# Identity transposes ahead of the first real ones, and one coefficient load on another queue

## The chip, the cores and the metric

The kernel runs on one core of a Trainium2 chip. The metric is device time in microseconds (us) of one execution. Before the change the median of three runs is 1470.12 us.

## What is computed

One layer of an encoder for two sequences of 512 tokens with 1024 features: a norm of the rows, a wide projection, a windowed attention branch, a state-space branch, a gated merge, and an MLP. Everything is in fp32. What the change touches is the beginning:

```python
def rms_norm(x, g):
    xf = x.astype(jnp.float32)
    y = xf * lax.rsqrt(jnp.mean(xf * xf, axis=-1, keepdims=True) + EPS)
    return (y * g.astype(jnp.float32)).astype(x.dtype)
...
    h = rms_norm(x, ln1)
    proj = h @ w_in
    q, k, v, u, g_att, g_ssm = jnp.split(proj, IN_SPLITS, axis=-1)
...
    a_re, a_im, bb_re, bb_im = s5_discretize(lam_re, lam_im, log_dt, b_re, b_im)
```

The state-space branch has 64 groups of 16 channels with 64 states in two directions. `s5_discretize` turns the decay rates `lam` and `log_dt` into powers and scale factors, which are then multiplied with the coefficients `b` and `c` of each group.

## The kernel before

The 1024 rows of x (both sequences) are eight tiles `xs[0]` to `xs[7]` of 128 rows by 1024 features, 512 KB each. SyncE (SP) issues their loads (L285), four of them, then the first two halves of a weight column (`fetch`, L165), then the other four.

**The front.** `square_rows(t)` squares a tile on ScalarE with a row sum (L290), and GpSimd turns the sum into the scale of each row (L292, L293). `scale_rows(t)` multiplies the rows on VectorE (L296). `turn_rows(s, k)` transposes the k-th 128 features of the four tiles of sequence s on TensorE into one PSUM tile (L301; tiles named `sps` and `tps` in turn), so that the features lie on the partitions. From that PSUM tile ScalarE writes a rounded copy `hT[s][0]` (L303), and VectorE writes what rounding left out, `hT[s][1]` (L304). Each product of the projection is then three matmuls per k (L185): rounded by rounded, rounded by rest, rest by rounded. `split` does the same rounding for a weight half, with a cast on ScalarE (L175, tile `c_hi`) and a subtraction on VectorE (L176, tile `c_lo`), and after the second half issues the next `fetch`.

**The order.** From L270 to L436 the instructions of all five engines keep the order in which the program writes them (`manual_schedule`). After L436 this holds for TensorE and GpSimd alone (L437), and the planner orders the others; it may also put their later instructions between earlier ones of the written order. Matmuls of the projection are handed out in small portions by `pull(units)`, two units each: three matmuls after each `turn_rows(0, k)` from k = 2 on, and larger portions later.

For the first sequence the loop over k reads:

```python
        for k in range(KT):
            turn_rows(0, k)
            if k % 2 == 0:
                square_rows(4 + k // 2)
            elif k > 1:
                scale_rows(3 + k // 2)
            if k in (4, 5):
                split(k - 4)
            if k > 1:
                pull(6)
```

So ScalarE and VectorE work on the transposed tiles of the first sequence and, in between, on the rows of the second one.

**The coefficients.** `coefficients()` is a long chain of small VectorE operations (L327 to L384), handed out by `some(n)` among the rest. Its results are copied into tables (L429 to L438). Then `tables(c)` runs for eight blocks c of eight groups. It loads the block's coefficients into `bcx` (L469, 256 KB, two buffers), multiplies them with the factors (L475 to L481), forms `bpre` (L504 to L507) and `ctab` (L528 to L532), lets TensorE transpose `bpre` (L517), and stores `ctab` through GpSimd's queue (L533). `h`, which holds the states, is a tile of the pool opened after the front's pools are closed; GpSimd clears its first step (L444) ahead of the first `tables`. GpSimd's written order around there is: the row scales (L292, L293), small operations on constants (L415 to L419), the store of a line of attention biases (L423), the clearing of `h` (L444), and the stores of `ctab` (L533).

**PSUM.** `acc()` gives one of three accumulator tiles in turn, `sps()` one of two, `tps()` one of two. `ident` is the 128 by 128 identity, made by GpSimd at the start.

Of the kernel before, what the change touches and what calls it, by code (L numbers as in the profile page):

```python
# [19 lines left out]
P = 128  # L20
# [43 lines left out]
def hybrid_layer(ctx, tc, x, rel, onehot, w_qkv, w_ug, vectors, lam, coefs, w_glu, w_out, ln2,  # L64
                 w_up, w_down, out):
    nc = tc.nc
    V, S, PE, GP, SP = nc.vector, nc.scalar, nc.tensor, nc.gpsimd, nc.sync
# [12 lines left out]
    def acc():  # L80
        return ps_acc.tile([P, 512], F32, tag="acc", name="acc")

    def tps():
        return ps_t.tile([P, 512], F32, tag="tps", name="tps")

    def sps():
        return ps_s.tile([P, 512], F32, tag="sps", name="sps")
# [16 lines left out]
    ident = const.tile([P, P], F32, name="ident")  # L104
# [166 lines left out]
    with tc.tile_pool(name="xin", bufs=1, reuse_waits="tile") as xin, tc.tile_pool(name="ssmc", bufs=1) as sc:  # L271
# [23 lines left out]
        def scale_rows(t):  # L295
            V.tensor_scalar_mul(xs[t], xs[t], scales[t])  # L296

        def turn_rows(s, k):
            ps = tps() if k % 2 else sps()
            for i in range(4):  # L300
                PE.transpose(ps[:, i * P:(i + 1) * P], xs[s * 4 + i][:, k * P:(k + 1) * P], ident)  # L301
            h = hT[s][0][:, k, :]
            S.activation(h, ps, AF.Copy, scale=gain_1[:, k:k + 1])  # L303
            V.scalar_tensor_tensor(hT[s][1][:, k, :], ps, gain_1[:, k:k + 1], h.bitcast(F32),  # L304
                                   op0=ALU.mult, op1=ALU.subtract)
# [93 lines left out]
# [10 lines that stand above are left out]
        scale_rows(7)  # L409
        pull(12)  # L410
        for k in range(KT):
            turn_rows(1, k)
            pull(6)
            some(4)
# [27 lines left out]
    with tc.tile_pool(name="hst", bufs=1) as hp:  # L442
# [11 lines left out]
        with tc.tile_pool(name="ssmt", bufs=2) as sp:  # L454
# [9 lines left out]
            def tables(c):  # L464


                gs = slice(c * SB, (c + 1) * SB)
                bcx = sp.tile([P, SB, 4, CH], F32, tag="bcx", name="bcx")
                SP.dma_start(bcx, coefs[:, gs])  # L469
                bcv = bcx.rearrange("p g i c -> p i g c")  # L470
                bx, cx = bcv[:, 0:2], bcv[:, 2:4]
                bb = sp.tile([P, 4, SB, CH], F32, tag="bb", name="bb", bufs=1)
# [105 lines left out]
            for c in range(KT):  # L578
                tables(c)
                if c == 1:  # L580
                    step_factors()
# [610 lines left out]
    with tc.tile_pool(name="glu", bufs=1, reuse_waits="tile") as gpool, \  # L1192
# [10 lines left out]
        for u in range(2, 2 * KT):  # L1203
            m, s = divmod(u, 2)
# [436 lines left out]
```

## Time and profile before

| what | us |
|---|---|
| median of three runs | 1470.12 |
| the three runs | 1469.74, 1470.12, 1473.99 |
| the profiled execution's own time | 1473.9 |
| its span (first to last instruction) | 1472.1 |
| VectorE busy | 1098.8 (75%) |
| ScalarE busy | 758.3 (52%) |
| GpSimd busy | 212.2 (14%) |

A row of the timeline reads: start in us from the start of the span, duration in us, engine, line, operation, what it writes and reads, shape, how many in a row, and in brackets how long the engine had been idle before and what released it. PE is TensorE's matmul, PEld its weight load, DVE VectorE, ACT ScalarE, POOL GpSimd, and SPq, ACTq, POOLq are instructions that issue a DMA. A row of the waits reads: who waited for whom, microseconds in total, how often, the longest. A row of the windows reads: the stretch, its length, the busy time of each engine with the number of instructions, the granted TensorE clock (PEclk), the share of the DMA engines and GB/s.

### The profile page before, as it was taken

The numbers are of one execution on the slowest core, as the hardware profiler recorded it, in microseconds if no ns is written. First come the engines' busy times: TensorE is split into PE (matmuls) and PEld (weight loads), VectorE is DVE, ScalarE is ACT, GpSimd is POOL, SyncE is SP. The second block draws the span as 40 slices with busy tenths as digits, with TensorE's granted clock in tenths as the row PEclk, the third lists the DMA queues.
The fourth block names the chain that finished last, engine by engine and source line by source line (L and its number), as shares of the span: only waits on it lengthen the run. The fifth ranks groups of instructions, "written<-read, shape, count | busy, mean of one in ns | idle before, by whom it ended". The sixth has DMA issues, their size and how long they took to land.

```text
span 1472.1 us, 22149 instructions
## 1 busy us (share of the span) xinstructions
PE 1441.2 (98%) x8074; PEld 1232.5 (84%) x8074; DVE 1098.8 (75%) x1989; ACT 758.3 (52%) x1362; POOL 212.2 (14%) x372
## 2 busy tenths in 40 slices
PE   6999999999999999999999999999999999999998
PEld 4888888888999999998888878888888878888787
DVE  7989849996645899998984587777776597475553
ACT  6678852235535888786343355544554444333332
POOL 3033351002331444232100000000000000000000
PEclk9999999999999999999999999999999999999999
DMA  4455549429840445376552245444443893454441
GB/s 177 140 172 180 167 159 347 144 100 315 316 163 16 149 147 170 99 243 228 190 193 107 86 160 177 146 154 146 145 148 113 327 341 104 158 185 146 127 129 58
DMA packets 102877, 249.16 MB, mean 169 GB/s; under 512 B 12234, under 2 KB 23754, under 8 KB 102768
## 3 DMA queue, kind: packets, MB, share of 16 engines
q1 hardware_dynamic: 60240, 139.55, 29.1%
q0 software_dynamic: 16896, 53.53, 10.7%
q10 hardware_dynamic: 25632, 54.67, 10.1%
q8 instruction: 64, 1.05, 0.3%
q14 instruction: 45, 0.37, 0.1%
HBM read 173.22 MB, written 90.21 MB: 179 GB/s over the span
## 4 chain that ended last, share of the span: by engine, by line
PE 75%; DVE 12%; DMA 4%; issue 4%; ACT 2%; POOL 2%; SPq 0%; ACTq 0%; DVEq 0%; POOLq 0%
PE bank L117 13%; PE bank L118 13%; PE bank L116 13%; PE acc L185 6%; PE acc L825 5%; PE acc L123 3%; PE acc L117 3%; PE acc L118 3%; PE acc L116 3%; PE po L908 2%; PE sps L876 2%; PE tps L892 2%; PE sps L546 2%; DMA c_raw<-in_w_ug_dram 2%; DVE t L614 1%
## 5 line engine op out<-in xcount | busy, mean ns | idle before, releaser
L185 PE MATMUL acc<-act,c_hi 128*128 128x512 f32 x768 | 245.0, 397 | 1.0 <-DVE act L304 1.0
L117 PE MATMUL bank<-b_lo,a_hi 128*128 128x512 f32 x448 | 174.7, 390 | 1.4 <-DVE b_lo L1510 1.4
L118 PE MATMUL bank<-b_hi,a_lo 128*128 128x512 f32 x448 | 174.3, 389 | 0.0
L116 PE MATMUL bank<-b_hi,a_hi 128*128 128x512 f32 x448 | 173.5, 389 | 0.0
L185 PEld LDWEIGHTS acc<-act,c_hi 128*128 128x128 f32 x768 | 143.4, 189 | 30.6 <-DVE act L304 2.4
L1509 ACT CAST a_hi<-d_a 128x1024 fp32r<-128x1024 f32 x56 | 59.0, 1053 | 179.8 <-PE bank L117 176.6
L185 PE MATMUL acc<-act,c_lo 128*128 128x512 f32 x384 | 151.2, 394 | 0.0
L116 PE MATMUL bank<-act,act 128*128 128x512 f32 x368 | 143.3, 389 | 0.5 <-ACT f_sum L1334 0.5
L117 PE MATMUL bank<-act,act 128*128 128x512 f32 x368 | 143.3, 389 | 0.2 <-DVE act L1293 0.2
L118 PE MATMUL bank<-act,act 128*128 128x512 f32 x368 | 143.2, 389 | 0.0
L1510 DVE TENSOR_TENSOR a_lo<-d_a,a_hi 128x1024 fp32r<-128x1024 f32 x56 | 68.5, 1223 | 99.9 <-ACT a_hi L1509 99.9
L825 PE MATMUL acc<-w_hi,act 128*128 128x256 f32 x512 | 114.2, 291 | 0.0
L117 PEld LDWEIGHTS bank<-b_lo,a_hi 128*128 128x128 f32 x448 | 84.1, 188 | 20.3 <-DVE b_lo L1510 2.9
L116 PEld LDWEIGHTS bank<-b_hi,a_hi 128*128 128x128 f32 x448 | 84.1, 188 | 17.5
L118 PEld LDWEIGHTS bank<-b_hi,a_lo 128*128 128x128 f32 x448 | 84.1, 188 | 17.3
L825 PEld LDWEIGHTS acc<-w_hi,act 128*128 128x128 f32 x512 | 87.1, 190 | 3.7
L185 PEld LDWEIGHTS acc<-act,c_lo 128*128 128x128 f32 x384 | 72.5, 189 | 14.7 <-DVE c_lo L176 0.5
L116 PEld LDWEIGHTS bank<-act,act 128*128 128x128 f32 x368 | 69.1, 188 | 15.1 <-ACT f_sum L1334 0.9
L117 PEld LDWEIGHTS bank<-act,act 128*128 128x128 f32 x368 | 69.1, 188 | 14.8 <-DVE act L1293 0.5
L886 ACT ACTIVATE p<-p,nmx 128x257 f32<-128x257 f32 (+1 forms) x128 | 72.1, 564 | 18.0 <-DVE nmx L880 16.7
L118 PEld LDWEIGHTS bank<-act,act 128*128 128x128 f32 x368 | 69.1, 188 | 14.4
L123 PE MATMUL acc<-act,gc_hi 128*128 128x512 f32 x256 | 80.8, 394 | 0.0
(332 smaller groups left out, 3421.7 us busy)
## 6 DMA issues: line engine op xcount, KB each, us to landing
d_a<-a_scr SPq DMA_DIRECT2D x56, 512.0 KB, 3.6
raws<-in_w_up_dram SPq DMA_DIRECT2D x32, 512.0 KB, 4.0
a_scr<-t ACTq DMA_DIRECT2D x64, 256.0 KB, 3.0
k<-in_w_down_dram SPq DMA_DIRECT2D x32, 512.0 KB, 6.2
c_raw<-in_w_ug_dram SPq DMA_DIRECT2D x48, 256.0 KB, 3.7
ct_scr<-ctab POOLq DMA_DIRECT2D x16, 576.0 KB, 3.6
ctab_in<-ct_scr POOLq DMA_DIRECT2D x16, 576.0 KB, 7.9
y_scr<-y_scr POOLq DMA_DIRECT2D x16, 512.0 KB, 5.6
```

The lines of the kernel that those rows point to most:

```text
L116: PE.matmul(ps, a[0], b[0], start=first, stop=False)
L117: PE.matmul(ps, a[0], b[1], start=False, stop=False)
L118: PE.matmul(ps, a[1], b[0], start=False, stop=last)
L123: PE.matmul(ps, w[wi][:, k, :], rows[yi], start=k + p == 0, stop=k == KT - 1 and p == 2)
L185: PE.matmul(ps, w[wi][:, k, :], hT[s][hi][:, k, :], start=n == 0, stop=n == 3 * KT - 1)
L546: PE.matmul(ps[:, i * P:(i + 1) * P], bm[:, ri, g, :], u_sb[:, gp * SH + g, :], start=True, stop=True)
L825: PE.matmul(self.ps, hT[sq][act][:, k, col:col + P], w[:, k % 4, :], start=i == 0, stop=i == 3 * KT - 1)
L876: PE.matmul(ps[:, 0:self.nk], qs, kk[:, self.k0 * P:self.k1 * P], start=i == 0, stop=i == 1)
L886: S.activation(p, p, AF.Exp, bias=self.nmx[:, h:h + 1], scale=-1.0, accum_out=self.sums[:, h, self.qb:self.qb + 1])
L892: PE.transpose(pt[:, h * P:(h + 1) * P], self.p[:, h, 1 + i * P:1 + (i + 1) * P], ident)
L1509: S.copy(hi, src)
L1510: V.tensor_sub(lo, src, hi.bitcast(F32))
```

## The change

Two edits. First, a PSUM tile `idle` is taken from the accumulators, and `busy(n)` writes n transposes of the identity into it, four places in turn; nobody reads it. In the very first `turn_rows` (s = 0, k = 0), 32 of them stand ahead of the transpose of `xs[0]`, and eight each ahead of those of `xs[1]`, `xs[2]` and `xs[3]`: 56 in all. Second, the load of `bcx` for c = 0 is issued by GpSimd instead of SP; the other seven stay on SP.

```diff
+        idle = acc()
+
+        def busy(n):
+            for i in range(n):
+                PE.transpose(idle[:, i % 4 * P:(i % 4 + 1) * P], ident, ident)
+
         def turn_rows(s, k):
             ps = tps() if k % 2 else sps()
             for i in range(4):
+                if s + k == 0:
+                    busy(8 if i else 32)
                 PE.transpose(ps[:, i * P:(i + 1) * P], xs[s * 4 + i][:, k * P:(k + 1) * P], ident)
             h = hT[s][0][:, k, :]
             S.activation(h, ps, AF.Copy, scale=gain_1[:, k:k + 1])
...
                 bcx = sp.tile([P, SB, 4, CH], F32, tag="bcx", name="bcx")
-                SP.dma_start(bcx, coefs[:, gs])
+                (SP if c else GP).dma_start(bcx, coefs[:, gs])
```

## Prediction

> **What bounds the kernel now.** I read the page first: the span, the engines, the slices.
>
> ```profile
> span 1472.1 us, 22149 instructions
> PE 1441.2 (98%) x8074; PEld 1232.5 (84%) x8074; DVE 1098.8 (75%) x1989; ACT 758.3 (52%) x1362; POOL 212.2 (14%) x372
> PE   6999999999999999999999999999999999999998
> ```
>
> TensorE is busy 98%, and all slices but the first and the last read 9. So a shift of TensorE's stream in the front runs through to the end, one for one, as long as what the later stages wait for is itself counted from that stream. By the code it is: the scan on VectorE and the loads behind it start from TensorE's products. What is open to the change is the first slice, 37 us. The waits of its first 30 us say where TensorE stood still:
>
> ```profile
> PE sps L301 <- DVE xt L296: 11.8, 5, 7.9
> ```
>
> TensorE waits for scaled rows. Its own timeline shows these waits, and a second thing:
>
> ```profile
> 7.92 0.47 PE L301 MATMUL sps<-ident,xt 128*128 128x128 f32 x1 [7.92 <-DVE xt L296]
> 9.44 0.47 PE L301 MATMUL sps<-ident,xt 128*128 128x128 f32 x1 [1.05 <-DVE xt L296]
> 11.36 0.47 PE L301 MATMUL sps<-ident,xt 128*128 128x128 f32 x1 [1.44 <-DVE xt L296]
> 12.93 0.48 PE L301 MATMUL sps<-ident,xt 128*128 128x128 f32 x1 [1.10 <-DVE xt L296]
> 13.20 1.06 PE L301 MATMUL tps<-ident,xt 128*128 128x128 f32 x4
> 14.05 1.06 PE L301 MATMUL sps<-ident,xt 128*128 128x128 f32 x4
> 17.11 1.03 PE L185 MATMUL acc<-act,c_hi 128*128 128x512 f32 x2
> 17.98 0.39 PE L185 MATMUL acc<-act,c_lo 128*128 128x512 f32 x1
> 18.21 0.60 PE L301 MATMUL sps<-ident,xt 128*128 128x128 f32 x4
> L301 PE MATMUL tps<-ident,xt x32: 270/272/421, 13.2 to 34.6; 128*128 128x128 f32 x32
> ```
>
> Four transposes last 1.06 us before 17.11 and 0.60 after 17.98. From start to start it is (14.05 - 13.20) / 4 = 0.213 us first; later, with 0.27 for one (the last row: shortest, median and longest in ns), (0.60 - 0.27) / 3 = 0.11. TensorE runs at half speed until about 17.9. The windows show the same change elsewhere (the clock column reads 1.00 at the start, so the durations decide there):
>
> ```profile
> 11.10:14.50 3.40, 2.04 (x9) 1.75 (x10) 2.96 (x10) 1.74 (x4) 0.90 (x2) 1.00 1.03 417
> 14.50:17.90 3.40, 3.40 (x12) 2.65 (x11) 2.64 (x6) 3.26 (x7) 1.16 (x4) 1.00 0.98 339
> 386.50:389.90 3.40, 1.24 (x11) 1.03 (x9) 3.13 (x6) 2.02 (x5) 2.40 (x3) 0.99 1.05 414
> 389.90:393.30 3.40, 3.21 (x15) 3.24 (x16) 0.80 (x2) 0.68 (x2) 0.00 (x0) 0.51 1.03 379
> 393.30:396.70 3.40, 3.40 (x32) 3.40 (x32) 1.02 (x3) 1.98 (x6) 1.86 (x3) 1.00 0.87 345
> ```
>
> After a stretch of 3.4 us with 1.24 us of TensorE work (36%) the clock is 0.51 for one such stretch, and a full one brings it back. In the front, 2.04 of 3.40 (60%) did not raise it and 3.40 of 3.40 did.
>
> **The change, part by part: the transposes.** GpSimd has the identity ready early:
>
> ```profile
> 1.02 0.28 POOL masks.py:199 TENSOR_SCALAR_AFFINE_SELECT ident<-ident 128x128 f32<-128x128 f32 x1
> ```
>
> From about 1.4 us, 32 transposes at the slow 0.213 last 6.8 us, to 8.2. That holds a whole stretch of 3.4 us wherever its border lies, so the clock rises between 4.8 and 8.2 if these transposes count as work; the rest then goes at 0.11, and the transpose of `xs[0]` (7.92) is at most 0.3 late. Eight more at 0.11 are 0.9 us, inside the waits of 1.05 to 1.44. Nothing that bounds 12.93 moves: rows, sums and scales do not come from TensorE. `idle` has no reader, and in the rotation of `acc` only TensorE's own order stands behind it, so it costs nothing; without that cover it would be one accumulator less, for which no wait is seen. From 8 to 13 us TensorE would be busy about 60%; the trace has no case between 36% (falls) and 100% (holds), and I take that it holds, since the gaps stay below 1.5 us where those above exceed 2.
>
> What a full clock at 12.93 is worth is read from ScalarE and VectorE, which take the tiles:
>
> ```profile
> 13.45 0.69 ACT L303 ACTIVATE act<-sps,vec 128x512 fp32r<-128x512 f32 x1 [1.66 <-PE sps L301]
> 17.16 0.21 ACT L290 ACTIVATION_READ_ACCUMULATOR rn_junk<-xt 128x1 f32 x1
> 17.50 0.69 ACT L303 ACTIVATE act<-tps,vec 128x512 fp32r<-128x512 f32 x1
> 18.85 0.69 ACT L303 ACTIVATE act<-sps,vec 128x512 fp32r<-128x512 f32 x1 [0.66 <-PE sps L301]
> 13.38 1.29 DVE L176 TENSOR_TENSOR c_lo<-c_raw,c_hi 128x512 fp32r<-128x512 f32 x2
> 14.59 0.74 DVE L304 SCALAR_TENSOR_TENSOR act<-sps,vec,act 128x512 fp32r<-128x512 f32 x1
> 25.08 1.41 DVE L296 TENSOR_SCALAR xt<-xt,rs 128x1024 f32<-128x1024 f32 x2
> ```
>
> ScalarE starts the first tile at 13.45 and has hardly a gap until it is through with the eighth. Its time lost to TensorE is 0.48 - 0.27 = 0.21 at the start, 17.50 - 17.37 = 0.13, and 0.66 at 18.85: 1.0 us. With the fast clock both later tiles are in time: the second matmul of a portion waits for VectorE's 14.59, which stays (the two subtractions at 13.38 stand before it), and then three matmuls and four transposes need about 1 us instead of 2. VectorE's last scaling of rows (25.08) comes 1.0 earlier, and with it TensorE's dense stretch. So **-1.0 us**. The ends: 0 if VectorE does not follow, -2.5 if half of the 5 us at half clock (12.93 to 17.9) were saved whole.
>
> A rule of the Trainium skill speaks against it. "TensorE: Matmul & The Clock Gate", Part 4, says that transposes do not count as busy for the clock in the way that matmuls do; Part 1 gives a window of about 3.4 us of sustained work, with which the stretches above agree. The 60% window that did not raise the clock held transposes almost alone, which fits that rule and fits a threshold above 60% as well. By the rule the sum of this part would be a loss, the second rival below.
>
> **The load.** Rows of the load (the first is of all `bcx` loads), of GpSimd's queue around the new place, and of the users; the last is GpSimd's nearest transfer, with its median time to landing:
>
> ```profile
> DMA to landing us min/median/max: 3.1/4.2/8.5
> 8.26 0.33 SPq L469 DMA_DIRECT2D bcx<-in_coefs_dram  x1
> 48.33 0.24 ACT L435 COPY er<-pr 128x64 f32<-128x64 f32 x1
> 48.64 0.31 POOL L444 MEMSET h<- 128x256 f32 x1 [10.63 <-DMA u_sb<-u_scr]
> 46.15 0.42 DVE L476 TENSOR_TENSOR bb<-bcx,fr 128x256 f32<-128x256 f32 x1
> 51.89 0.68 DVE L504 TENSOR_TENSOR tb<-bs_p,bb 128x512 f32<-128x512 f32 x1
> 55.45 0.68 DVE L507 TENSOR_TENSOR bpre<-tb,bpre 128x512 f32<-128x512 f32 x1
> 50.00:60.00 10.00, 9.65 (x46) 7.54 (x45) 9.54 (x19) 6.75 (x24) 0.22 (x1) 1.00 0.41 133
> 56.19 0.88 PE L517 MATMUL tps<-ident,bpre 128*128 128x128 f32 x6 [0.32 <-DVE bpre L507]
> 59.78 0.60 POOL L533 DMA_DIRECT2D ct_scr<-ctab  x1 [10.83 <-DVE ctab L532]
> 66.95 0.42 DVE L476 TENSOR_TENSOR bb<-bcx,fr 128x256 f32<-128x256 f32 x1
> 68.84 0.69 DVE L504 TENSOR_TENSOR tb<-bs_p,bb 128x512 f32<-128x512 f32 x1
> ct_scr<-ctab POOLq DMA_DIRECT2D x16, 576.0 KB, 3.6
> ```
>
> On SP the load goes out at 8.26, among the rows. Taking its 256 KB out of there (0.7 us at the 339 to 417 GB/s of the windows) frees transfers that nobody waits for: ScalarE's stops after 13.45 are on TensorE. Nothing on SP is held up by it or let go by it.
>
> On GpSimd the written order puts it behind the clearing of `h` (L444), which runs at 48.64, right after the last read of the front's tables at 48.33 + 0.24 (the page names a DMA that ends at the same time). The load would go out at 48.95. Landing takes 3.1 to 4.2 by its own rows; I take 3.6, the row of GpSimd's queue: 52.55. From L476 to L504 a later block needs 68.84 - 66.95 = 1.89, so L504 starts at 54.4 instead of 51.89. From there five operations at a pitch of about 0.6 and the last one's 0.68 end at 57.5 instead of 55.45 + 0.68 = 56.13. TensorE waits just there for L507: **+1.4 us**; with 3.1 and the two unneeded operations put off +0.5, with 4.2 and the subtraction of a weight half in between +2.6. Behind the load in GpSimd's queue is the store of `ctab` at 59.78, which nobody waits for soon.
>
> The sum is -1.0 + 1.4 = **+0.4 us**. It is made on the profiled execution (1473.9 own time, 1472.1 span, 1.8 around it), 3.8 above the median of 1470.12; I carry it to the median: **1470.5 us**.
>
> **The rivals.**
>
> 1. The load is in time: the order of GpSimd is not as I read it, or other VectorE work fills the wait. For it: VectorE is busy 9.54 of the 10 us from 50 to 60, so it has other work to put there. Against: L444 is ahead in the written order. Then only -1.0: 1469.1.
>
> 2. Transposes do not raise the clock, so the change does not do what it is written for. 32 at 0.213 end at 8.2; each real one and the eight after it are 9 x 0.213 = 1.9 against gaps of 1.5 to 1.9. The fourth real one starts at 1.4 + 59 x 0.213 = 13.97 instead of 12.93, 1.0 late; half of that comes back when the clock rises at 17.9 as before. So +0.5 to +1.0, with the load about +2.2: 1472.3. For it: the 60% window; against: those transposes had gaps between them. The page cited above states this rule.
>
> 3. On the slower side: the load lands late enough to drop the clock. Each microsecond above 3.6 is one more on TensorE. From some 2.2 us of wait within a stretch (389.90's case) a half-clock stretch follows, 1.7 us. At a landing of 5.6 it is +1.4 + 2.0 + 1.7 - 1.0 = +4.1, 1474.2; at 8.5, the longest landing of a `bcx` load, +7.0, 1477.1. Against: the 8.5 was among the rows, and the DMA share from 50 to 60 us is 0.41.
>
> **How the numbers follow.** About 0.3%, 4.4 us, is what a measurement of this kernel can tell from no change. Forecast 0.42, first rival 0.22, second 0.25, third 0.08, and 0.03 for the planner ordering VectorE better by more than I can see. The first three lie within 4.4 us; of the third over half is outside: slower 0.06, faster 0.03, same 0.91. The range takes in the bounds of the load and the clock, -2.5 + 0 and +2.6 with the second rival's +1.0: 1467.0 to 1474.0.
>
> **What would show it.** Right: transposes of `idle` at 0.11 from before 8.2; four real ones in 0.60 at 13.2; L303 without the 0.66; the last L296 near 24; `bcx` issued by POOL behind L444; TensorE's wait for L507 grown from 0.3 to about 1.7. Wrong: 0.213 throughout, the fourth transpose near 14, `bcx` issued before 40 us, or a wait at L517 above 3 us.

## The result, and the profile after

| | before | after |
|---|---|---|
| median, five runs of each, us | 1470.12 | 1478.51 |
| lowest to highest, us | 1468.35 to 1476.57 | 1477.4 to 1480.92 |
| the profiled execution's own time, us | 1473.9 | 1478.51 |
| its span, us | 1472.1 | 1476.7 |

The ratio is 1.0044, with an interval of 1.0028 to 1.0061: **slower by 4.1 to 9.0 us**, outside the predicted range. Of all executions in this document two ran at a mean granted clock of 0.56 and 0.66 (2416.55 us among those of the early load, 2057.06 us among those of before in one group), and the ratios leave them out. The page's first lines after the change:

```profile
span 1476.7 us, 22263 instructions
PE 1447.6 (98%) x8130; PEld 1239.3 (84%) x8130; DVE 1099.4 (74%) x1989; ACT 758.7 (51%) x1362; POOL 212.8 (14%) x373
```

TensorE has 56 matmuls more, the transposes of `idle`. From here on, lines of the kernel after L308 are those of before plus 8 (L304 is now L312, L507 is L515, L517 is L525). TensorE's timeline after the change, in time order:

```profile
1.36 5.56 PE L302 MATMUL acc<-ident 128*128 128x128 f32 x32 [1.36 <-POOL ident masks.py:199]
...
12.71 0.33 PE L309 MATMUL sps<-ident,xt 128*128 128x128 f32 x1 [0.38 <-DVE xt L296]
12.88 0.60 PE L309 MATMUL tps<-ident,xt 128*128 128x128 f32 x4
...
25.22 0.33 PE L309 MATMUL sps<-ident,xt 128*128 128x128 f32 x1 [0.26 <-DVE xt L296]
...
57.45 2.15 PE L525 MATMUL tps<-ident,bpre 128*128 128x128 f32 x8 [3.45 <-DVE bpre L515]
...
67.12 1.95 PE L554 MATMUL sps<-u_sb,bm 128*128 128x128 f32 x16
```

The front does what the first edit is for: the 32 transposes last 5.56 us and not 6.8, and the four real ones at 12.88 last 0.60 as they do at full clock. The other end of the list is the loss: TensorE stands still for 3.45 us ahead of the first transposes of `bpre`, and those are slow (eight last 2.15 us; the next eight, at 68.91, last 1.04). Three rows of before mark the same places there:

```profile
26.55 0.33 PE L301 MATMUL sps<-ident,xt 128*128 128x128 f32 x1 [0.27 <-DVE xt L296]
...
55.49 0.38 PE L517 MATMUL tps<-ident,bpre 128*128 128x128 f32 x2
...
62.85 1.95 PE L546 MATMUL sps<-u_sb,bm 128*128 128x128 f32 x16
```

So against this execution of before the stream is 1.33 us ahead at the last scaled rows (25.22 against 26.55) and 4.27 us behind at the first product with `u_sb` (67.12 against 62.85). With the matmuls of both traces laid side by side in their order, the distance then stays at 4.28 until 317 us, and the end is 4.6 later. What follows is hence about 25 to 67 us. VectorE's timeline in that stretch:

```profile
52.25 0.43 DVE L483 TENSOR_TENSOR tw<-bcx,fi 128x256 f32<-128x256 f32 x1 [2.73 <-DMA bcx<-in_coefs_dram]
...
54.09 0.69 DVE L176 TENSOR_TENSOR c_lo<-c_raw,c_hi 128x512 fp32r<-128x512 f32 x1
54.70 0.28 DVE L489 TENSOR_TENSOR bb<-bb 128x128 f32<-128x128 f32 x1
54.91 0.69 DVE L512 TENSOR_TENSOR tb<-bs_p,bb 128x512 f32<-128x512 f32 x1
...
56.71 1.29 DVE L515 TENSOR_TENSOR bpre<-tb,bpre 128x512 f32<-128x512 f32 x2
```

VectorE waits 2.73 us for the load. Then a weight half's subtraction (`c_lo`, 54.09) stands in its order between two operations on `bb`, and the last subtraction of `bpre` ends at 56.71 + 1.29 = 58.00. The subtraction needs ScalarE's cast of the same half, which itself waits for a weight load and ends at 53.44 + 0.62 = 54.06:

```profile
53.44 0.62 ACT L175 CAST c_hi<-c_raw 128x512 fp32r<-128x512 f32 x1 [3.40 <-DMA c_raw<-in_w_ug_dram]
```

In VectorE's order of before the third such subtraction of this stretch stands behind the operations on `bb`, between the two L507, and costs 0.46 us of waiting:

```profile
54.84 0.69 DVE L176 TENSOR_TENSOR c_lo<-c_raw,c_hi 128x512 fp32r<-128x512 f32 x1 [0.46 <-ACT c_hi L175]
```

The new place of the load has thus changed what stands ahead of `bpre`. The issues of GpSimd (the first row) and of SP (the other two):

```profile
47.59 0.61 POOL L477 DMA_DIRECT2D bcx<-in_coefs_dram  x1
```

```profile
46.24 0.50 SPq L477 DMA_DIRECT2D bcx<-in_coefs_dram  x1
48.77 1.50 SPq L165 DMA_DIRECT2D c_raw<-in_w_ug_dram  x2
```

The load of c = 0 goes out at 47.59 and is read at 52.25, 4.66 us later. Just ahead of it now stands the load of c = 1 on SP, and just behind it two weight halves. In SP's order of before the load of c = 1 was at another place:

```profile
15.07 0.42 SPq L469 DMA_DIRECT2D bcx<-in_coefs_dram  x1
```

The planner moved it from 15.07 to 46.24; the diff does not touch it. Last, the windows of after around the clock's changes (stretch, its length, busy time of PE, PEld, DVE, ACT, POOL, then the granted clock; it reads 1.00 ahead of the first change, so there durations decide):

```profile
1.78:5.20 3.42, 3.42 (x18) 3.42 (x17) 0.34 (x2) 2.00 (x3) 1.97 (x3) 1.00 0.97 328
8.60:12.00 3.40, 2.26 (x19) 1.84 (x18) 2.36 (x9) 2.90 (x6) 1.87 (x4) 1.00 1.05 404
53.00:56.40 3.40, 1.00 (x5) 0.50 (x3) 3.32 (x11) 2.90 (x9) 0.00 (x0) 1.00 0.20 73
56.40:59.80 3.40, 2.35 (x9) 1.96 (x10) 3.40 (x6) 2.19 (x10) 0.00 (x0) 0.50 0.08 31
59.80:63.20 3.40, 3.40 (x9) 2.64 (x8) 2.75 (x5) 0.42 (x1) 0.55 (x1) 0.50 0.14 57
63.20:66.60 3.40, 3.40 (x16) 2.78 (x15) 1.58 (x3) 1.63 (x3) 0.00 (x0) 1.00 0.38 150
```

The wait leaves TensorE 1.00 of 3.40 us of work from 53.0 on. The clock then falls to 0.50 and stays there for **two** stretches, 6.8 us: the first has 2.35 us of work, which does not raise it, and only the second, full one does.

The 4.27 us divide as follows. The first edit gives 1.33 back. The first transpose of `bpre` begins at 57.45; in before the first of the eight began at 55.49 (the row of two), so up to here 1.96 are lost, and the wait alone has cost 1.96 + 1.33 = 3.29. From there to 67.12 another 4.27 - 1.96 = 2.31 are lost, at half clock. Before has its own wait of 0.32 in this part (56.19, in the prediction), which the new kernel does not have there; counted without it, the half clock took 2.63 and the wait 2.97.

### The profile page after: what moved, and what is told of

The parts are those of the page before. It is cut to its first block, busy times and chain, and to the rows that moved or that the text cites. A ratio compares the mean times of both kernels' runs of the same rounds, so it can differ in the third digit from the quotient of the medians.

```text
span 1476.7 us, 22263 instructions
## 1 busy us (share of the span) xinstructions
PE 1447.6 (98%) x8130; PEld 1239.3 (84%) x8130; DVE 1099.4 (74%) x1989; ACT 758.7 (51%) x1362; POOL 212.8 (14%) x373
## 4 chain that ended last, share of the span: by engine, by line
PE 63%; DVE 11%; issue 5%; DMA 3%; ACT 2%; POOL 1%; ACTq 0%; POOLq 0%; DVEq 0%; SPq 0%
PE bank L117 14%; PE bank L118 13%; PE bank L116 13%; PE acc L833 5%; PE acc L123 3%; PE po L916 2%; PE sps L884 2%; DMA c_raw<-in_w_ug_dram 2%; PE tps L900 2%; PE acc L117 2%; PE acc L118 2%; PE acc L116 1%; DVE t L622 1%; DVE h L625 1%; DVE t L624 1%
```

## The experiments

All ten kernels compute the whole layer. Those in one group share the runs of before on one chip (medians 1471.7, 1472.7 and 1471.82). Their edits shift the lines behind them by a few more (L515 of after is L517 in some rows). Where the expectations speak of a theory A, it is the account above: the transposes gain, and the load costs through the wait and the half clock. B and others are its rivals, as each text states them. What is read from a profile is one execution of a kernel.

### Each edit alone

The transposes, with the load back on SP:

```diff
-                (SP if c else GP).dma_start(bcx, coefs[:, gs])
+                SP.dma_start(bcx, coefs[:, gs])
```

> The 56 identity transposes without the moved load. Theory A (the loss is the place of the load): TensorE's dense stream near 50 us runs 1.2 to 1.4 us earlier than in the kernel before, the wait at L517's transposes stays at 0.3, the clock shows no half stretch before 300 us; the time is 1468.5 to 1470, a ratio of 0.999. Theory B (the loss comes with the transposes: a shifted stream, an accumulator fewer): the loss is here, 1474 or more.

Measured: median 1476.6, ratio 1.0034 (1.0022 to 1.0045). Slower: A's number fell and B's came, though not for B's reasons (a shifted stream, an accumulator fewer). VectorE's timeline of this kernel shows why, and beside it is the same operation in before:

```profile
16.55 0.29 DVE L488 TENSOR_TENSOR cw<-bcx 128x128 f32<-128x128 f32 x1 [1.94 <-DMA bcx<-in_coefs_dram]
16.76 0.74 DVE L312 SCALAR_TENSOR_TENSOR act<-sps,vec,act 128x512 fp32r<-128x512 f32 x1
```

```profile
16.45 0.74 DVE L304 SCALAR_TENSOR_TENSOR act<-sps,vec,act 128x512 fp32r<-128x512 f32 x1
17.11 0.28 DVE L480 TENSOR_TENSOR cw<-bcx 128x128 f32<-128x128 f32 x1
```

In before, this sum over the block's coefficients stands at 17.11, behind the third L304. With transposes added on TensorE, the planner puts it ahead of the *first* one. Its load was issued at 8.27, among the rows of x, and arrives at about 16.5. VectorE waits 1.94 us, the first L312 starts at 16.76 instead of 14.59, and TensorE waits for that. TensorE's row, and the windows around it:

```profile
17.56 0.80 PE L185 MATMUL acc<-act,c_hi 128*128 128x512 f32 x1 [3.08 <-DVE act L312]
```

```profile
13.80:17.30 3.50, 0.68 (x4) 0.22 (x2) 1.56 (x4) 3.35 (x7) 0.85 (x3) 0.99 0.97 350
17.30:20.70 3.40, 3.14 (x9) 2.48 (x10) 2.03 (x5) 0.69 (x1) 0.74 (x2) 0.50 0.21 76
```

TensorE waits 3.08 us, and the clock that the transposes had raised falls to 0.50 for one stretch.

The load alone, with before's front:

```diff
-                SP.dma_start(bcx, coefs[:, gs])
+                (SP if c else GP).dma_start(bcx, coefs[:, gs])
```

> The kernel before with only the first coefficient load moved to GpSimd. Theory A: the load goes out behind the clearing of h near 49 us, VectorE waits for it, TensorE's wait at the transposes of bpre grows from 0.3 to 3 us or more, a stretch of 3.4 to 6.8 us at half clock follows, and the stream is 5 to 6.5 us later from there on; the time is 1475 to 1477. Theory B: within 1 us of the kernel before.

Measured: median 1477.18, ratio 1.0038 (1.0023 to 1.0054), slower as A has it, and just above A's 1475 to 1477. TensorE's rows and the windows:

```profile
57.87 2.14 PE L517 MATMUL tps<-ident,bpre 128*128 128x128 f32 x8 [3.28 <-DVE bpre L507]
...
67.62 1.95 PE L546 MATMUL sps<-u_sb,bm 128*128 128x128 f32 x16
```

```profile
53.60:57.00 3.40, 0.99 (x5) 0.49 (x3) 2.53 (x6) 3.09 (x9) 0.00 (x0) 1.00 0.24 85
57.00:60.40 3.40, 2.53 (x10) 2.13 (x11) 3.40 (x7) 2.19 (x9) 0.00 (x0) 0.50 0.07 19
60.40:63.80 3.40, 3.40 (x10) 2.63 (x9) 2.56 (x5) 0.23 (x1) 0.55 (x1) 0.50 0.20 81
```

The same wait, the same two stretches, without any transposes in the front. So each edit loses when it is alone, 4.9 and 5.5 us by the medians. Together they do not lose by both mechanisms, since the second edit takes away what makes the first one lose: with the load on GpSimd the sums over `bcx` leave the front, and the changed kernel has no wait for them there.

### The transposes without the moved operation

To see the first edit by itself, the load stays on SP, and for c = 0 four operations are held at their written place, the two that had moved (`cw`) and the same two on `bb`:

```diff
-                    V.tensor_add(dst[:, 0], src[:, 0], src[:, 1])
-                    V.tensor_sub(dst[:, 1], src[:, 0], src[:, 1])
+                    put = V.tensor_add(dst[:, 0], src[:, 0], src[:, 1])
+                    if c == 0:
+                        tc.keep_in_program_order(put)
+                    put = V.tensor_sub(dst[:, 1], src[:, 0], src[:, 1])
+                    if c == 0:
+                        tc.keep_in_program_order(put)
```

> The 56 transposes without the moved load, and the two operations that write cw for the first block held at their place in the written order on VectorE (behind the first operations on bb). If the loss of the transposes alone comes from VectorE waiting for bcx at those two operations near 14.6 us: no wait for bcx there, TensorE's wait of 3.1 near 14 us falls to 1.0 or less, no half clock near 17 us, and the stream at 50 us is 1.2 to 1.5 us earlier than in the kernel before; the time is within 2 us of the kernel before, 4 below the transposes alone. If the transposes themselves cost (an accumulator fewer, a shifted stream): it stays 4 to 5 us above.

Measured: median 1473.4, ratio 1.0009 (0.9998 to 1.0020): no difference that the interval shows. VectorE's and TensorE's timelines:

```profile
14.62 0.74 DVE L312 SCALAR_TENSOR_TENSOR act<-sps,vec,act 128x512 fp32r<-128x512 f32 x1
```

```profile
61.77 1.95 PE L558 MATMUL sps<-u_sb,bm 128*128 128x128 f32 x16
```

The wait and the half clock of the transposes alone are gone, and the loss falls from 4.9 us to 0.7, each by the medians against before in its own group. The moved operation is thus shown to be the loss of that run. A gain in time is not shown.

### The load ahead of the clearing of `h`

The load is held ahead of the clearing in GpSimd's written order, and the clearing comes behind it:

```diff
-            GP.memset(h[:, 0], 0.0)
...
-                (SP if c else GP).dma_start(bcx, coefs[:, gs])
+                got = (SP if c else GP).dma_start(bcx, coefs[:, gs])
+                if c == 0:
+                    tc.keep_in_program_order(got)
+                    GP.memset(h[:, 0], 0.0)
```

> The changed kernel with the first coefficient load put ahead of the clearing of h in GpSimd's written order, behind the store of the attention line (issued near 36.5 us instead of 47.6). Theory A: it lands near 41 us, before its first use near 45; TensorE's wait at the transposes of bpre is below 0.8, no half clock there, and the stream is 1.0 to 1.4 us earlier than in the kernel before; 1468.5 to 1470. Theory B: as the changed kernel, 1476 or more. A third: it is GpSimd's queue that is slow, whatever the place; then the load lands after 46 us and a wait stays.

Measured: median 1473.42, ratio 1.0008 (0.9997 to 1.0018); the loss is gone, but the 1468.5 to 1470 that A had did not come. GpSimd's row and TensorE's:

```profile
36.75 0.61 POOL L476 DMA_DIRECT2D bcx<-in_coefs_dram  x1
```

```profile
55.07 0.87 PE L527 MATMUL tps<-ident,bpre 128*128 128x128 f32 x6 [0.79 <-DVE bpre L517]
...
61.69 1.95 PE L556 MATMUL sps<-u_sb,bm 128*128 128x128 f32 x16
```

With the load 10.84 us earlier (36.75 against 47.59) the wait falls from 3.45 to 0.79, and the stream at the product with `u_sb` is at 61.69 instead of 67.12. So the place behind L444 is the loss, by 5.4 us of the stream and 5.1 of the medians (1478.51 and 1473.42, of two groups). This edit takes away two things at once, the late load and, since the planner's whole order is another one, the weight half that is not ready ahead of `bpre`.

### The half clock apart from the wait

The changed kernel as it is, with 30 transposes of the identity on TensorE in the time that it would wait:

```diff
+                        if c + q + gp == 0:
+                            fill = acc()
+                            for i in range(30):
+                                PE.transpose(fill[:, i % 4 * P:(i % 4 + 1) * P], ident, ident)
```

> The changed kernel with 30 more identity transposes on TensorE just ahead of the first transposes of bpre, where it waits (3.3 us of work at 0.11 each). Separates the wait from the clock. If the half clock after the wait is a loss of its own: the wait for bpre ends at the same time (transposes start near 57.5), the clock stays full, and from 64 us on the stream is about 2 us behind the kernel before instead of 4; the time is 2 to 2.5 us below the changed kernel, 1475 to 1476.5. If the half clock costs nothing of its own: no difference from the changed kernel.

Measured: median 1475.14, ratio 1.0024 (1.0014 to 1.0034). TensorE's timeline and a window:

```profile
54.08 3.44 PE L527 MATMUL acc<-ident 128*128 128x128 f32 x30
57.77 0.44 PE L529 MATMUL tps<-ident,bpre 128*128 128x128 f32 x2 [0.26 <-DVE bpre L515]
...
65.00 1.95 PE L558 MATMUL sps<-u_sb,bm 128*128 128x128 f32 x16
```

```profile
56.40:59.80 3.40, 2.98 (x23) 2.38 (x22) 3.40 (x7) 2.74 (x12) 0.00 (x0) 1.00 0.17 64
```

The transposes of `bpre` begin no earlier (57.77 against 57.45), but the clock stays at 1.00, and the product with `u_sb` begins at 65.00 instead of 67.12. The half clock is a loss of its own of 2.1 us on the stream, and 2.4 counted from the first of these transposes (from there to the product it is 7.23 us instead of 9.67); the wait's 3.3 remain. The medians differ by 3.4 (1478.51 and 1475.14, of two groups), more than the 2 to 2.5 expected; the runs do not show where the rest comes from.

### What ends the wait

Was the late landing the doing of the load of c = 1, which now goes out 1.35 us ahead on SP? Here it is held at its written place, and goes out at 69.34:

```diff
-                (SP if c else GP).dma_start(bcx, coefs[:, gs])
+                got = (SP if c else GP).dma_start(bcx, coefs[:, gs])
+                if c == 1:
+                    tc.keep_in_program_order(got)
```

> The changed kernel with the second block's coefficient load held at its place in SP's written order, so that it no longer goes out at 46.2 us, 1.4 us ahead of the first block's load. If that transfer made the first load land 4.7 us after its issue instead of about 3.6: the landing is 3.4 to 3.8 us, TensorE's wait at the transposes of bpre falls from 3.5 to about 2.4, and the stream from 70 us on is 2.5 to 3.5 us behind the kernel before instead of 4.3. If the landing is that of GpSimd's queue or of the weight columns under way: the landing stays at 4.5 us or more and nothing changes.

Measured: median 1479.75, ratio 1.0053 (1.0035 to 1.0071); no better than after. VectorE's and TensorE's timelines:

```profile
51.09 0.43 DVE L485 TENSOR_TENSOR tw<-bcx,fi 128x256 f32<-128x256 f32 x1 [1.56 <-DMA bcx<-in_coefs_dram]
...
55.02 0.69 DVE L176 TENSOR_TENSOR c_lo<-c_raw,c_hi 128x512 fp32r<-128x512 f32 x1 [2.16 <-ACT c_hi L175]
```

```profile
58.37 2.14 PE L527 MATMUL tps<-ident,bpre 128*128 128x128 f32 x8 [4.38 <-DVE bpre L517]
```

Alone, the load is read 3.5 us after its issue, and VectorE begins at 51.09 instead of 52.25. That the other load had delayed it is still not shown: in the changed kernel with later transposes (the last experiment), whose front is the same code, the load of c = 1 goes out 1.68 us ahead too (45.84 and 47.52), and the load of c = 0 is read at 51.19, 3.67 us after its issue. In any case the gain does not reach TensorE. In VectorE's order the weight half's subtraction stands ahead of the last operation on `bb`, and its own data is late, so VectorE stands 2.16 us there. The first `bpre` has two gates, the coefficients and a weight half, and to open one brings out the other.

All five kernels whose load stands behind the clearing of `h` have this order on VectorE. Their times, in us of each profiled execution:

| kernel | `bcx` read | cast `c_hi` ends | `c_lo` starts | last `bpre` ends |
|---|---|---|---|---|
| after | 52.25 | 54.06 | 54.09 | 58.00 |
| after, TensorE filled | 52.21 | 54.38 | 54.41 | 58.32 |
| the load alone | 51.87 | 54.48 | 54.51 | 58.41 |
| after, later transposes | 51.19 | 54.86 | 54.90 | 58.79 |
| after, load of c = 1 held | 51.09 | 54.99 | 55.02 | 58.91 |

The subtraction starts 0.03 to 0.04 us after the cast in all five, and `bpre` is done 3.9 us after that, however early the coefficients are read. So in this order the weight half ends the wait, in after by a small margin (the operation on `bb` ahead of it ends at 54.01). No run holds this subtraction back by itself; this is read from five traces and not tested by an edit.

### Later stretches kept busy

The last question was why two versions without the wait (the early load, and the transposes with the operation held) are not below before in time. In the profiled execution of before the clock fell twice later on (389.9 is in the prediction). Four kernels got 22 and 18 transposes of the identity ahead of the two waits there: before, the changed kernel, the early load, and the transposes with the operation held.

```diff
+                if q in (12, 24):
+                    keep = acc()
+                    for i in range(22 if q == 12 else 18):
+                        PE.transpose(keep[:, i % 4 * P:(i % 4 + 1) * P], ident, ident)
```

> The kernel before with 22 and 18 identity transposes on TensorE ahead of the two batches of the state-space output that wait for their table (waits of 3.2 and 2.4 us near 358 and 390). If half clocks after these two waits make most of the spread of the kernel before (1468.5 to 1475): no half clock between 350 and 400 us, all runs within 2.5 us of each other, median 1468 to 1470. If the spread has another source, it stays at 6 us.

> The changed kernel with the same work at the two later waits. If its loss is made near 55 us (3.3 us of wait and about 3.4 of half clock, less the 1.35 gained before): 5 to 6 us above the kernel before with the same work there, 1473.5 to 1475.5. If part of the loss is made by more half clocks at the two later waits: less than 4 above it.

> The transposes with the load ahead of the clearing of h, and the same work at the two later waits. With the later half clocks out of the way the 1.2 to 1.4 us that TensorE's stream gains by 50 us should be seen in the time: 1467 to 1469, about 1.3 below the kernel before with the same work there. If the gain is given back at a wait that does not move (the tables' loads), it equals that kernel within 0.5.

> The transposes alone with the two cw operations held at their written place, and the work at the two later waits: the first edit with both of its losses out of the way and SP's load as before. TensorE's stream is 1.2 to 1.5 us ahead of the kernel before at 50 us, with no half clock between 20 and 1400 us; the time is 1469 to 1471.5, some 2 us below the kernel before, as for the kernel with the early load. If that kernel owed its time to the place of the load, this one is not below the kernel before.

| with the later transposes | median, us | ratio to before |
|---|---|---|
| before | 1473.15 | 1.0001 (0.9990 to 1.0013) |
| the changed kernel | 1476.54 | 1.0028 (1.0016 to 1.0039) |
| early load | 1470.62 | 0.9990 (0.9979 to 1.0001) |
| transposes, operation held (a later group on the same chip) | 1471.43 | 0.9994 (0.9984 to 1.0004) |

The windows of before with them, in the two places:

```profile
357.40:360.80 3.40, 3.40 (x28) 3.19 (x27) 1.93 (x4) 1.32 (x4) 0.00 (x0) 1.00 1.04 381
389.40:392.80 3.40, 3.40 (x32) 3.40 (x31) 0.68 (x2) 2.06 (x6) 1.58 (x3) 1.00 1.02 384
```

The clock no longer falls there, yet before is no faster, and my expectation of 1468 to 1470 for it missed. Its runs spread less: 12 of them over 3.4 us (1471.43 to 1474.83) with a standard deviation of 1.15, against 2.01 for the 34 of before in the group. The other three spread less too (1.33, 0.99 and 1.01, against 1.72, 1.74 and 1.70 without the later transposes), which speaks for those half clocks as a part of what sets the time from run to run, though they do not set the median of before.

The changed kernel is 3.4 us over before with the same transposes. Expected were 5 to 6 if the loss is made near 55 us, and less than 4 if part of it is made by later half clocks; by that mark a part is. Yet the streams of these two executions are 5.7 us apart at the product with `u_sb` (67.81 and 62.07), and at 317 us still. So the loss arises near 55 us, and the later waits change how much of it is left at the end; by how much in the median, one profile of each does not tell.

The early load is 2.5 us below before with the same transposes, 12 runs of each, which is clear of the spread of both (0.99 and 1.15), though above its expected 1467 to 1469. But its interval against before itself reaches 1.0001, so **no version is shown to be faster than before**.

These runs also give the front of before twice more. TensorE's timelines of before with the later transposes, and of the load alone, both with before's front:

```profile
25.77 0.33 PE L301 MATMUL sps<-ident,xt 128*128 128x128 f32 x1 [0.27 <-DVE xt L296]
...
62.07 1.95 PE L546 MATMUL sps<-u_sb,bm 128*128 128x128 f32 x16
```

```profile
25.81 0.33 PE L301 MATMUL sps<-ident,xt 128*128 128x128 f32 x1 [0.27 <-DVE xt L296]
```

The execution of before that the prediction read had 26.55 here. The same code reached the point 0.7 us earlier in both others, because its clock went up earlier: the slow matmuls end by about 16.4 and 16.0 there, and not at 17.9. In the kernels with the first edit and no wait in the front the point lies between 25.14 and 25.45, eight executions in all, 0.3 to 1.4 earlier. A part of that is rows of x which came a little earlier or later. From the fourth real transpose (12.93 in before, 12.71 in after) to this point the eight need 12.49 to 12.51 us and the three 13.62, 13.09 and 12.70. So the first edit is worth **0.2 to 1.1 us**, by where the clock's stretches happened to begin in the execution of before. With the load in time, the product with `u_sb` begins between 61.61 and 61.80 in four kernels, against 62.07 and 62.85 in before: 0.3 to 1.2.

## Why the prediction was wrong

**The transposes: right.** -1.0 was forecast. Measured against the same execution it is -1.33, of which 0.22 is rows that came earlier (12.71 for 12.93), so -1.1. The forecast is right for the execution that it was read from; against the other two fronts of before the edit is worth 0.6 and 0.2. Each sign that was named came: 32 in 5.56 us, the four real ones in 0.60, the last L296 early (VectorE), and ScalarE's fifth tile without the 0.66:

```profile
23.76 1.41 DVE L296 TENSOR_SCALAR xt<-xt,rs 128x1024 f32<-128x1024 f32 x2
```

```profile
17.52 0.69 ACT L311 ACTIVATE act<-sps,vec 128x512 fp32r<-128x512 f32 x1
```

The second rival, transposes that do not raise the clock, is refuted: the stretch from 1.78 to 5.20 holds nothing else (3.42 of 3.42), and the clock is up after it. The rule of the Trainium skill, "TensorE: Matmul & The Clock Gate", Part 4, that transposes do not count as busy for the clock in the way that matmuls do, is not borne out by this trace. These are fp32 transposes and stand in the trace as MATMUL; whether they are the kind that the rule means, no run here shows. That about 60% holds the clock was taken without a case, and 2.26 of 3.40 (66%) held it.

**What was missed beside it.** The prediction says that "nothing on SP is held up by it or let go by it", and it takes the order on VectorE as unchanged. Neither holds. The planner moved the load of c = 1 from 15.07 to 46.24, and with the first edit alone it moves the sum over `bcx` ahead of the first L304. The prediction costed the instructions of the diff; the loss came through instructions that the diff does not name.

**The load: the step that failed.** "+1.4 us" is the term that was mis-sized. 3.29 was measured at the first transpose of `bpre`, and 3.20 at the prediction's own mark, the end of the last subtraction (58.00 against 56.13 - 1.33 = 54.80). TensorE's wait of 3.45 is also the sign of being wrong that the prediction names, one above 3 us. The issue came as the step has it: 47.59 instead of 48.95, earlier by about what the front gained.

Along VectorE's order the excess of 1.8 has two parts. The load was read 4.66 us after its issue and not 3.6, the figure of GpSimd's nearest row: 1.06. And from the first operation on `bcx` to L512 VectorE took 54.91 - 52.25 = 2.66 us and not 1.89: 0.77, all of it the weight half's subtraction, since the two sums over `bcx` are in the 1.89 as well. The upper end of +2.6 allowed for the weight half, but not for a landing above 4.2, nor for a weight half that comes late itself.

The second part is the one that decides. The prediction took the stretch from L476 to L504 from a later block, in which no weight half stands. In the order that came out one does, its cast ends at 54.06, and the five executions above show that a landing of 3.5 or 3.7 us would not have let `bpre` be done any earlier.

**The half clock: the rival that decided.** The third rival had the mechanism right, that a wait above 2.2 us within a stretch drops the clock: TensorE was idle 3.40 - 1.00 = 2.40 us from 53.0 to 56.4. It failed on where it starts and what it costs. By the step's own numbers the wait is 1.7 us at a landing of 3.6, so 2.2 is reached at 4.1, inside the range already taken for the load; it was weighed at 5.6 and 8.5 instead, with a chance of 0.08. And it was priced at one stretch, 1.7 us; two ran at half clock and cost 2.31 on the stream, because the first one after the wait was not full.

**The sum.** -1.33 + 3.29 + 2.31 = +4.27 on the stream, against +0.4. The profiled executions differ by 4.6 and the medians by 8.4, because the profiled execution of before was 3.8 above its median; the interval of 4.1 to 9.0 holds both. Left open is the time of the versions without the wait: their streams are 0.3 to 1.2 us ahead at 62 us, and their medians without the later transposes are 0.7 and 1.7 above before's, with intervals of the ratio that hold 1. With them they are 0.4 and 2.1 below before of their groups, while before itself is 0.5 above, so by the medians the later half clocks cost these two more than they cost before. Single later waits also differ from one execution to the next (TensorE's wait for `rn_xn` is 0.7 us in before, 1.7 in after and 2.5 in before with the later transposes), and the runs do not tell whether an earlier stream makes them longer.

## What to carry to other kernels

Where a planner orders an engine, cost a change by the whole order that comes out, not by its own lines: two harmless edits each made it put an operation that waits for a transfer ahead of the one that TensorE needed. Before a load is moved from where it is early to where it is just in time, count what stands between its landing and what the bottleneck reads, and what each of these operations waits for itself; and add the half clock as soon as the wait comes near 2.2 us in a stretch of 3.4 (1.2 us of idle time did not drop the clock here). And a clock raised earlier was worth 1.1 us or next to nothing here, by the moment in which the stretches begin, so it takes several profiled executions of the same code to size it.

## What the runs showed of the hardware

- fp32 transposes of an identity alone brought TensorE to its faster clock: from 1.78 to 5.20 us it did nothing else (3.42 of 3.42), and the 32 last 5.56 us where 32 at the slow pitch of 0.213 are 6.8.
- To raise the clock took more than to hold it. Stretches with 2.04, 2.35 and 2.53 of 3.40 us of work (60%, 69%, 74%) did not raise it, and one with 3.14 (92%) did; those with 2.26 and 2.17 (66%, 64%; after, from 8.60 and 12.00) held it; those with 1.24, 1.00, 0.99 of 3.40 and 0.68 of 3.50 dropped it.
- A 256 KB load through GpSimd's queue, with two weight halves issued from 1.18 us behind it on, was read 4.66, 4.41, 3.68 and 3.67 us after its issue with another 256 KB load 1.35, 1.04, 2.21 and 1.68 us ahead of it, and 3.49 us after without that load, each in one execution.
